# Attention scores of two heads as alternating 64-row fp32 matmuls, with queries and keys kept as one fp32 copy

## The chip, the cores and the metric

The kernel runs on one core of one Trainium2 chip. The metric is the device time of one execution in microseconds (us). Five engines work beside each other, each through its own queue in order: TensorE (PE in the profile; its weight loads are shown apart as PEld), VectorE (DVE), ScalarE (ACT), GpSimd (POOL) and SyncE (SP, which only issues DMA transfers here). They wait for one another by semaphores.

## The reference, cut to what matters

One inference step of a decoder layer: a normalised input is projected by one matrix, its columns are split into a mixer A (windowed attention, 6 heads of 64) and a mixer B (mLSTM, 4 heads of 160), the two outputs go through one output projection, and a feed-forward network follows. 2048 prompt positions and 8 single-token samples are computed. The change touches mixer A on the prompt:

```python
s = jnp.einsum('bnqrhe,bnkrhe->bnrhqk', qb, kc).astype(jnp.float32) * scale + bias
s = jnp.where(mask[None, :, None, None], s, NEG)
lse = jax.nn.logsumexp(s, axis=-1)
p = jnp.exp(s - lse[..., None]).astype(v.dtype)
o = jnp.einsum('bnrhqk,bnkrhe->bnqrhe', p, vc).reshape(B, s_pad, H, E)[:, :S]
...
o = jnp.stack([b[0] for b in branches])
w = jax.nn.softmax(lse, axis=0).astype(o.dtype)
return jnp.einsum('gbsh,gbshe->bshe', w, o)
```

Every head is computed for three branches, (window, dilation) = (128, 1), (512, 4) and (2048, 16). In each, 128 queries that lie `dilation` positions apart see the 128 keys of their own block and, where there is one, the 128 keys of the block before. All inputs and outputs are fp32.

## The kernel before

The program is recorded in Python and a list scheduler then puts each engine's instructions into a fixed order, by priority and by its own estimate of when operands are ready. So work of several stages is interleaved on PE, but the order is fixed when the program is built. The stages that matter:

- **Normalisation and values** (`norm_and_v`, L770): tile by tile, x is normalised and transposed, and the value columns and gates are projected. The values go to a DRAM buffer `v_d` laid out head by head, with a column of ones behind each head's 64 (L863).
- **Projection of keys and queries** (`project_qk`, L909): for each of three column blocks (two heads each) and six blocks of positions, 24 matmuls on split operands (`mm3`, L161: a high and a low fp32r part of each operand) fill a PSUM tile `pmm`. The tile is copied to `qb` by ACT, and split again into `qhi` (ACT) and `qlo` (DVE, L159 for keys, L956 for queries). Each goes to its own DRAM buffer (L962). Keys are also transposed (`to_rows`, L913) for the output `p_k` through a tile `kt`. Between the column blocks, `setup_bias` (L235) writes the bias table to DRAM by a broadcast to 128 rows (L252), and `setup_gates` (L260) makes the gate sums; its PE transpose of `u` (L284) needs DVE's `u` (L282).
- **Second half of the projection for mixer B with attention** (`xbob(1)`, L1160): for each of its 15 blocks, six steps of the generator `attention` are recorded. PE's projection matmuls here are the groups called `pmm` at L162 to L164.
- **mLSTM with attention** (`mlstm`, L1167): 16 chunks, each a chain through PE, DVE, ACT and POOL; attention's remaining steps are recorded between them by a fixed ratio (L1229). When attention is done, the output weights are loaded there too.
- **Output projection and feed-forward network** (`phase_c`), after 1060 us, not touched.

Attention before works on one head at a time. `load_head` (L1042) loads `Q2`, which holds the high parts of a head's 64 query columns in rows 0 to 63 and the low parts in rows 64 to 127; `KH` and `KL`, which hold the high (low) parts of its keys twice. `front` (L1058) makes scores for two query blocks of the head: for each, two fp32r matmuls over all 128 rows and 256 columns, Q2 with KH and Q2 with KL, which add up in `ps_s` (L1073). The fp32r form is run with 256 columns even where only 128 keys count. For the branches with dilation 4 and 16 both operands are read with that stride. DVE adds the bias and takes the row minimum (L1075), ACT takes the exponential (L1077). `turn` (L1080) transposes the 128x128 blocks on PE, `weigh` (L1094) multiplies them with the values into `po`, ACT copies `po` to a row tile `R4` (L1103), and SP stores it. In what follows a **head-tile** is the scores of 128 queries of one head in one branch: 6 heads x 3 branches x 16 = 288 of them, 576 matmuls. `ps_s` has two buffers of one PSUM bank, each with two head-tiles.

fp32 matmuls stand in the profile as two PE records each (and two weight loads); fp32r matmuls and transposes as one.

## Time and profile before

| what | value |
|---|---|
| time, median of 3 runs | 2720.37 us (2719.04 to 2722.34) |
| span of the profiled execution | 2721.4 us |
| busy share of PE, DVE, ACT, POOL | 97%, 54%, 31%, 7% |
| matmul records at L1073 (scores) | 576, from 400.8 to 938.7 us |
| matmul records at L1101 (weighing with values), L1086 (transposes) | 900 and 450 |
| DMA packets | 334227, of these 108543 under 512 B |

The profiled execution's own time is taken as its span of 2721.4 us; it lies 1.0 us above the median of the three runs. A matmul's recorded duration reaches into the next ones, since matmuls are pipelined, so what one costs is read from the distance between the starts of successive records, not from its duration.

### The profile page before, as it was taken

To read this page: it belongs to the slowest core of one execution; us is meant where nothing else is said; L and a number is where in the kernel's file an instruction comes from. 1 tells how busy PE (TensorE), PEld (TensorE's weight loads), DVE (VectorE), ACT (ScalarE), POOL (GpSimd) and SP (SyncE) were. 2 spreads that over 40 slices of the span, in tenths; PEclk is the share of its full clock that TensorE was granted. 3 is DMA by queue.
4 is the path that set the end of the run, shared out by engine and by line. 5 is a ranking of instruction groups with operands and counts; after the bars stand their busy time and mean duration, and the time that the engine had idled before them with its cause. 6 is when DMAs were issued, how large, how long until landed. Compare 5 with 4: busy or idle time off the path is not lost.

```text
span 2721.4 us, 39886 instructions
## 1 busy us (share of the span) xinstructions
PE 2650.5 (97%) x15366; PEld 2355.4 (87%) x15366; DVE 1469.2 (54%) x3444; ACT 846.1 (31%) x1898; POOL 202.7 (7%) x198
## 2 busy tenths in 40 slices
PE   8999999999999979999999999999999999999997
PEld 7999999999798867887888888888899999999996
DVE  6324655666477575753344444544754545454547
ACT  5321224444445443322321212121452121212123
POOL 1000000000344243110000000000000000000001
PEclk9999999999799979999999999999999999999998
DMA  8675566656476565543222312111241111111113
GB/s 196 152 196 163 167 171 142 152 140 159 129 185 169 145 189 159 174 152 125 70 97 66 101 63 62 46 55 40 93 155 55 39 55 39 55 40 55 40 38 119
DMA packets 334227, 302.57 MB, mean 111 GB/s; under 512 B 108543, under 2 KB 301467, under 8 KB 331092
## 3 DMA queue, kind: packets, MB, share of 16 engines
q1 hardware_dynamic: 332212, 296.39, 38.6%
q0 software_dynamic: 1536, 3.10, 0.5%
q8 instruction: 121, 1.98, 0.3%
q14 instruction: 70, 0.57, 0.1%
q10 hardware_dynamic: 288, 0.53, 0.1%
HBM read 220.94 MB, written 95.17 MB: 116 GB/s over the span
## 4 chain that ended last, share of the span: by engine, by line
PE 88%; DVE 4%; DMA 4%; ACT 2%; issue 1%; POOL 1%; SPq 0%; DVEq 0%; POOLq 0%; ACTq 0%
PE pf L163 19%; PE pf L162 19%; PE pf L164 19%; PE pmm L162 5%; PE pmm L164 5%; PE pmm L163 5%; PE ps_s L1073 4%; PE po L1101 3%; PE pt L1086 2%; PE ptp L176 1%; PE ppq L162 1%; PE up L437 1%; DMA tr_d<-tb_d 0%; PE ppq L164 0%; PE nu L458 0%
## 5 line engine op out<-in xcount | busy, mean ns | idle before, releaser
L1442 DVE TENSOR_TENSOR acc<-acc,pf 128x512 f32<-128x512 f32 (+2 forms) x600 | 343.1, 581 | 201.5 <-PE pf L164 200.2
L164 PE MATMUL pf<-rh,w2l 128*128 128x512 f32 (+2 forms) x1280 | 445.4, 348 | 0.0
L163 PE MATMUL pf<-rlo,w2h 128*128 128x512 f32 (+2 forms) x1280 | 445.0, 348 | 0.1
L162 PE MATMUL pf<-rh,w2h 128*128 128x512 f32 (+2 forms) x1280 | 444.4, 347 | 0.0
L162 PEld LDWEIGHTS pf<-rh,w2h 128*128 128x128 f32 x1280 | 241.8, 189 | 30.2 <-ACT rh L158 0.2
L163 PEld LDWEIGHTS pf<-rlo,w2h 128*128 128x128 f32 x1280 | 241.4, 189 | 30.6 <-DVE rlo L159 0.3
L164 PEld LDWEIGHTS pf<-rh,w2l 128*128 128x128 f32 x1280 | 241.3, 189 | 30.0 <-DVE w2l L159 0.2
L162 PE MATMUL pmm<-x,wh 128*128 128x344 f32 (+1 forms) x768 | 251.3, 327 | 0.0
L163 PE MATMUL pmm<-x,wh 128*128 128x344 f32 (+1 forms) x768 | 249.3, 325 | 0.0
L164 PE MATMUL pmm<-x,wl 128*128 128x344 f32 (+1 forms) x768 | 248.7, 324 | 0.0
L162 PE MATMUL pf<-h21h,w1h 128*128 128x512 f32 (+2 forms) x768 | 245.8, 320 | 0.0
L164 PE MATMUL pf<-h21h,w1l 128*128 128x512 f32 (+2 forms) x768 | 245.6, 320 | 0.0
L163 PE MATMUL pf<-h21l,w1h 128*128 128x512 f32 (+2 forms) x768 | 245.2, 319 | 0.0
L158 ACT ACTIVATE rh<-rl 128x264 fp32r<-128x264 f32 (+1 forms) x160 | 87.1, 545 | 465.9 <-PE pf L164 278.9
L163 PE MATMUL pf<-h20l,w1h 128*128 128x512 f32 x512 | 200.0, 391 | 0.0
L162 PE MATMUL pf<-h20h,w1h 128*128 128x512 f32 x512 | 199.9, 390 | 0.0
L164 PE MATMUL pf<-h20h,w1l 128*128 128x512 f32 x512 | 199.4, 390 | 0.0
L159 DVE TENSOR_TENSOR w1l<-w1r,w1h 128x1024 fp32r<-128x1024 f32 x64 | 78.4, 1225 | 184.7 <-ACT w1h L158 184.7
L1077 ACT ACTIVATE ex<-sm,R 128x256 f32<-128x256 f32 (+1 forms) x288 | 125.9, 457 | 145.4 <-DVE R L1075 140.9
L1421 DVE TENSOR_TENSOR rl<-rl 128x264 f32<-128x264 f32 (+1 forms) x160 | 93.2, 583 | 141.4 <-ACT rl L1420 141.4
L1075 DVE CUSTOM_DVE_ANT_0 sm<-ps_s,nb 128x256 f32<-128x256 f32 (+1 forms) x288 | 99.7, 362 | 118.4 <-PE ps_s L1073 88.9
L163 PEld LDWEIGHTS pf<-h21l,w1h 128*128 128x128 f32 x768 | 144.6, 188 | 12.8
(471 smaller groups left out, 5171.0 us busy)
## 6 DMA issues: line engine op xcount, KB each, us to landing
w1r<-in_w_ff_dram SPq DMA_DIRECT2D x64, 512.0 KB
w2r<-in_w_ff_dram SPq DMA_DIRECT2D x64, 512.0 KB
xt<-in_x_prompt_dram SPq DMA_DIRECT2D x31, 512.0 KB
xt<-x_d SPq DMA_DIRECT2D x25, 512.0 KB
R_d<-R SPq DMA_DIRECT2D x72, 132.0 KB
Rb<-R_d SPq DMA_DIRECT2D x48, 198.0 KB
V<-v_d SPq DMA_DIRECT2D x72, 130.0 KB
wraw<-in_w_in_dram SPq DMA_DIRECT2D x17, 512.0 KB
```

Of the source, the lines that this page charges most:

```text
L158: last_hi[0] = act.activation(hi, src, AF.Copy)
L159: last_lo[0] = (eng or vec).tensor_tensor(lo, src, hi.bitcast(F32), op=OP.subtract)
L162: pe.matmul(out, lh, rh, start=first, stop=False)
L163: pe.matmul(out, lh, rl, start=False, stop=False)
L164: pe.matmul(out, ll, rh, start=False, stop=last)
L1073: pe.matmul(out, Q[:, a:a + (P - 1) * d + 1:d], mv, start=i == 0, stop=i == 1)
L1075: vec.tensor_tensor_reduce(sm[:, :w], s_[:, e, c0:c0 + w], nb[:, o + bw - w:o + bw], 1.0, 3e38, OP.add, OP.min, mn)
L1077: act.activation(ex[:, e, :w], sm[:, :w], AF.Exp, bias=mn, scale=-1.0)
L1086: pe.transpose(pt[:, e, kb], ex[:, e, kb * P:(kb + 1) * P], ident)
L1101: pe.matmul(po[:, i + e], pT[:, e, kb], vts[kb], start=kb == 0, stop=kb == nk - 1)
L1421: vec.tensor_tensor(r[:, :n], r[:, :n], r[:, :n], op=OP.mult)
L1442: vec.tensor_tensor(av, av, pf[:, :n], op=OP.add)
```

## The change

Queries and keys are no longer split for attention. `project_qk` copies each PSUM block once (queries with the scale -0.125) and stores it once, in one fp32 buffer `q_d` and one `k_d`. Their 128 rows per column block are two heads, 64 rows each. Attention takes the two heads of a column block as a pair: `load_pair` loads both heads' rows as they lie. For each query block, one fp32 matmul over rows 0 to 63 makes the first head's scores and one over rows 64 to 127 the second head's. The two write different PSUM banks, and they are recorded alternately. The matmuls have 128 columns where only 128 keys count, else 256. All 288 head-tiles are now one fp32 matmul each, 288 in place of 576.

A step makes two query blocks of two heads, in two `ps_s` buffers, so both buffers are taken in every step. `flush` is now a generator: it does one head of the pair, yields, and does the other. The lag between scores and transposes is one step (`DEPTH` 1) of double size. Values lie position by position in `v_d`, so that a pair's columns are read as pieces of 520 B; results are stored per step as pieces of 528 B in place of 264 B. The number of DVE, ACT and PE instructions per head-tile behind the scores stays as it was.

```diff
-    q_d = [dram.tile([DA, S], F32, name=f"q{x}_d") for x in "hl"]
-    k_d = [dram.tile([DA, S], F32, name=f"k{x}_d") for x in "hl"]
-    v_d = dram.tile([HA, S, HD + 1], F32, name="v_d")
+    q_d = dram.tile([DA, S], F32, name="q_d")
+    k_d = dram.tile([DA, S], F32, name="k_d")
+    v_d = dram.tile([S, VW], F32, name="v_d")
...
-                    hi = ev.tile([P, 344], F32R, name="qhi")
-                    lo = ev.tile([P, 344], F32R, name="qlo")
-                    if which == "k":
-                        qb = ev.tile([P, 344], F32, name="qb", bufs=3)
-                        act.activation(qb[:, :n], ps[:, :n], AF.Copy)
-                        split(hi[:, :n], lo[:, :n], qb[:, :n])
-                    else:
-                        act.activation(hi[:, :n], ps[:, :n], AF.Copy, scale=-0.125)
-                        vec.scalar_tensor_tensor(lo[:, :n], ps[:, :n], -0.125, hi[:, :n].bitcast(F32),
-                                                 op0=OP.mult, op1=OP.subtract)
...
-                    for dd, tt in zip(dst, (hi, lo)):
-                        nc.sync.dma_start(dd[j * P:(j + 1) * P, b0:b0 + m], tt[:, :m].bitcast(F32))
+                    qb = ev.tile([P, 344], F32, name="qb", bufs=3)
+                    act.activation(qb[:, :n], ps[:, :n], AF.Copy, scale=1.0 if which == "k" else -0.125)
+                    nc.sync.dma_start(dst[j * P:(j + 1) * P, b0:b0 + m], qb[:, :m])
...
-            Q, KH, KL = (wk.tile([P, S], F32, name=x) for x in ("Q2", "KH", "KL"))
-            for dst, lo, hi in ((Q, q_d[0], q_d[1]), (KH, k_d[0], k_d[0]), (KL, k_d[1], k_d[1])):
-                nc.sync.dma_start(dst[:HD], lo[hs])
-                nc.sync.dma_start(dst[HD:], hi[hs])
+            Q, K = (wk.tile([P, S], F32, name=x) for x in ("Q2", "K2"))
+            nc.sync.dma_start(Q, q_d[j * P:(j + 1) * P])
+            nc.sync.dma_start(K, k_d[j * P:(j + 1) * P])
...
-            s_ = ps.tile([P, 2, 256], F32, name="ps_s", tag="s", bufs=2)
-            for e, (a, w, mn, vts) in enumerate(tiles):
-                for i, K in enumerate((KH, KL)):
...
-                    pe.matmul(out, Q[:, a:a + (P - 1) * d + 1:d], mv, start=i == 0, stop=i == 1)
+            s_ = [ps.tile([P, 2, 256], F32, name="ps_s", tag="s", bufs=2) for _ in range(2)]
+            for t, (a, w, _, _) in enumerate(tiles):
+                k0 = a - (w - P) * d
+                for e in range(2):
+                    hs = slice(HD * e, HD * e + HD)
+                    pe.matmul(s_[e][:, t, :w], Q[hs, a:a + (P - 1) * d + 1:d],
+                              K[hs, k0:k0 + (w - 1) * d + 1:d], start=True, stop=True)
...
-        pend, turned, acc_o, DEPTH = [], [], [None], 2
+        nxt = load_pair(0)
+        pend, turned, acc_o, DEPTH = [], [], [None], 1
...
-                    V = wk.tile([P, 4, HD + 1], F32, name="V", bufs=4)
-                    nc.sync.dma_start(V, rows(v_d, b, g, HD + 1, h * S * (HD + 1), HD + 1))
-                    R4 = wk.tile([P, 4, HD + 2], F32, name="R4", bufs=3)
+                    V = wk.tile([P, 4, 2, HD + 1], F32, name="V", bufs=4)
+                    nc.sync.dma_start(V.rearrange("p t e c -> p t (e c)"),
+                                      rows(v_d, b, g, 0, VW, 2 * j * (HD + 1), 2 * (HD + 1)))
                     for i in (0, 2):
+                        R2 = wk.tile([P, 2, 2, HD + 2], F32, name="R2", bufs=4)
```

Where this moves instructions is shown in three places. The first is PE's queue in the stage where attention runs beside the projection for mixer B. Before, in the first head's steps with dilation 4, score matmuls (L1073) stand in pairs of KH and KL between projection matmuls (`pmm`) and transposes (`pt`):

```order
L1073 MATMUL ps_s<-KH,Q_4213 128x256
L1073 MATMUL ps_s<-KL,Q_4213 128x256
L1086 MATMUL pt<-ident,ex 128x128 x4
L163 MATMUL pmm<-x_115,wh 128x344
L1073 MATMUL ps_s<-KH,Q_4213 128x256
L1073 MATMUL ps_s<-KL,Q_4213 128x256
L164 MATMUL pmm<-x_114,wl 128x344
L1073 MATMUL ps_s<-KH,Q_4213 128x256
L1073 MATMUL ps_s<-KL,Q_4213 128x256
L1086 MATMUL pt<-ident,ex 128x128 x4
```

With the change, in the first pair's steps with dilation 4, four score matmuls (now L1055, two query blocks of two heads) stand together, and the steps follow each other in bursts, with transposes (L1072) and value matmuls (`po`, L1087) between:

```order
L1055 MATMUL ps_s<-K_4065,Q_4064 128x256 x4
L1087 MATMUL po<-V,pT 128x65 x4
L1072 MATMUL pt<-ident,ex 128x128 x4
L1087 MATMUL po<-V,pT 128x65 x4
L1072 MATMUL pt<-ident,ex 128x128 x4
L1055 MATMUL ps_s<-K_4065,Q_4064 128x256 x4
L1087 MATMUL po<-V,pT 128x65 x4
L1072 MATMUL pt<-ident,ex 128x128 x4
```

What moved: the score matmuls of a step now form one run, with nothing of another form in it. In all, the projection stage (up to PE's last `pmm` matmul) has 49 such runs with 168 score matmuls in place of 336, 128 of them with strided operands; 27 of the runs are a full alternation of four.

The second place is PE's queue in the mLSTM stage, in the last pair, where the scheduler could not keep the four together (`up`, `psA` and `pt<-ident,cp` are the mLSTM's own):

```order
L1055 MATMUL ps_s<-K_6769,Q_6768 128x256
L416 MATMUL pt<-ident,cp 128x128 x4
L1055 MATMUL ps_s<-K_6769,Q_6768 128x256
L418 MATMUL pt<-ident,cp 128x128
L1072 MATMUL pt<-ident,ex 128x128 x2
L1055 MATMUL ps_s<-K_6769,Q_6768 128x256
L437 MATMUL up<-v_7214,cw 128x161 x3
L439 MATMUL up<-v_7214,cw 128x161
L441 MATMUL up<-v_7214,cw 32x161 x4
L1055 MATMUL ps_s<-K_6769,Q_6768 128x256
```

What moved: here a 64-row matmul stands alone between others four times in one step. This stage has 54 runs with 120 score matmuls (64 strided) in place of 240; 12 runs are a full alternation, and 21 are a single matmul.

The third place is DVE's queue in the projection of keys, ahead of `u`. Before, four low parts (`qlo`) stand between the gates' `lf` and the copies that `u` needs:

```order
L330 SCALAR_TENSOR_TENSOR lf<-gat,ls_ab 128x64
L159 TENSOR_TENSOR qlo<-qb,qhi 128x340 x2
L159 TENSOR_TENSOR qlo<-qb,qhi 128x344 x2
L280 COPY a<-ptp 128x64
L281 COPY bt<-ptp 128x64
L282 TENSOR_TENSOR u<-gat,a 128x64
```

With the change nothing stands between them:

```order
L327 SCALAR_TENSOR_TENSOR ls_ab<-gat 128x64
L933 COPY qs_1478<-ptp 8x128
L330 SCALAR_TENSOR_TENSOR lf<-gat,ls_ab 128x64
L280 COPY a<-ptp 128x64
L281 COPY bt<-ptp 128x64
L282 TENSOR_TENSOR u<-gat,a 128x64
```

What moved: `u` no longer stands behind `qlo`, which is gone.

More of the change, by code (lines that the diff above doesn't have):

```diff
@@ L862, in norm_and_v @@
             if t < NT:
[L863 removed]
+                nc.sync.dma_start(v_d[c0:c0 + P], vt.rearrange("p h e -> p (h e)"))
                 nc.sync.dma_start(O["p_v"][0, 0, c0:c0 + P], vt[:, :, :HD])
@@ L1060, in front, with rows @@
+        def rows(t, b, g, i, rs, off, w):
+            st = ((rs, P * rs), (4 * rs, rs), (16 * rs, rs))[b]
+            row = (512 * g + P * i, 512 * g + i, 4 * g + i)[b]
+            n = 4 if t is v_d else 2
+            return bass.AP(tensor=t.tensor, offset=t.offset + row * rs + off, ap=[[st[0], P], [st[1], n], [1, w]])
+        def front(pair, b, tiles):
+            nb, Q, K = pair
             d = BRANCHES[b][1]
             o, bw = NBW[b]
-            ex = wk.tile([P, 2, 256], F32, name="ex", bufs=3)
@@ L1097, in weigh @@
             po = acc_o[0]
[L1098 removed]
+            for t, (_, w, _, vts) in enumerate(tiles):
                 nk = w // P
                 for kb in range(nk):
[L1101 to L1107 removed]
@@ L1109, in flush @@
-        def flush():
-            if len(turned) == 1:
-                weigh(*turned.pop(0))
-            if pend:
-                tiles, ex, *rest = pend.pop(0)
-                turned.append((tiles, turn(tiles, ex), *rest))
-        for h in range(HA):
-            cur = hd
+                    pe.matmul(po[:, t, e], pT[:, t, kb], vts[kb][:, e], start=kb == 0, stop=kb == nk - 1)
+            if e:
+                act.activation(R2[:, :, :, :HD + 1], po, AF.Copy)
+                nc.sync.dma_start(dst, R2.rearrange("p t e c -> p t (e c)"))
@@ new lines, in attention @@
+        nxt = load_pair(0)
+        pend, turned, acc_o, DEPTH = [], [], [None], 1
+        def flush():
+            old = turned.pop(0) if turned else None
+            new = pend.pop(0) if len(pend) > DEPTH or not live[0] and pend else None
+            pTs = []
+            for e in range(2):
+                if old is not None:
+                    tiles, pT, *rest = old
+                    weigh(tiles, pT[e], e, *rest)
+                if new is not None:
+                    pTs.append(turn(new[0], new[1], e))
+                if e == 0:
+                    yield
+            if new is not None:
+                turned.append((new[0], pTs, *new[2:]))
```

83 lines of the change are left out of this document (34 added, 49 removed).

## Prediction

> **What bounds the kernel now.** I read the page's busy shares first, then its chain of waits, then a table by stage.
>
> ```profile
> PE 2650.5 (97%) x15366; PEld 2355.4 (87%) x15366; DVE 1469.2 (54%) x3444; ACT 846.1 (31%) x1898; POOL 202.7 (7%) x198
> ...
> PE 88%; DVE 4%; DMA 4%; ACT 2%; issue 1%; POOL 1%; SPq 0%; DVEq 0%; POOLq 0%; ACTq 0%
> ```
>
> PE is busy 97% of the span and carries 88% of the chain: time is mostly PE's. The table by stage (columns: stretch, its length, busy time and count on PE, PEld, DVE, ACT, POOL, then the granted clock, DMA share, GB/s) has the projections up to 398 in two pieces, then attention beside the projection for mixer B (398 to 658), then attention inside the mLSTM (658 to 945).
>
> ```profile
> core 0: us, PE busy (x) PEld busy (x) DVE busy (x) ACT busy (x) POOL busy (x), PEclk, DMA share, GB/s
> 130.00:200.00 70.00, 64.30 (x402) 61.33 (x401) 21.30 (x78) 20.92 (x61) 1.13 (x5) 0.95 0.73 189
> 200.00:398.00 198.00, 197.25 (x1295) 196.29 (x1294) 109.49 (x258) 47.50 (x90) 0.00 (x0) 1.00 0.57 164
> 398.00:658.00 260.00, 259.76 (x1705) 251.25 (x1704) 156.79 (x600) 108.61 (x257) 0.95 (x3) 1.00 0.65 150
> 658.00:945.00 287.00, 271.79 (x1849) 242.47 (x1846) 185.44 (x599) 135.96 (x405) 104.67 (x96) 0.93 0.61 158
> ```
>
> In the first attention stage PE is idle 0.2 us of 260: what PE saves there is saved whole. In the second it is idle 15 of 287, at a mean clock of 0.93, so something else also sets the end. The chain of the first attention stage, by line and with one of its longest pieces:
>
> ```profile
> by line: PE ps_s L1073 31.5%; PE po L1101 19.0%; PE pmm L163 12.9%; PE pmm L164 12.8%; PE pmm L162 12.8%; PE pt L1086 10.5%; DVE g1t L1028 0.5%; PE ptp L1011 0.2%; issue 0.2%; DVE R L1075 0.0%; DVE sm L1075 0.0%
> 457.77 1.51 PE po L1101 x14
> ```
>
> Scores (L1073) are 31.5% of 260 us, 82 us. Their records in the two stages:
>
> ```profile
> 398.00:658.00 260.00, 104.18 (x338) 77.59 (x338) 1.00 0.65 150
> 658.00:945.00 287.00, 78.77 (x238) 52.85 (x238) 0.93 0.61 158
> ```
>
> 338 records are 169 head-tiles of two matmuls, so 0.48 us each. What a pair costs depends on its operands. First a pair with neighbouring columns (dilation 1), then two pairs with a stride, from the timeline of PE (start, duration, instruction, count):
>
> ```profile
> 449.03 0.33 PE L1101 MATMUL po<-V,pT 128*128 128x65 f32 x2
> 449.17 0.36 PE L1073 MATMUL ps_s<-KH,Q 128*128 128x256 f32 x1
> 449.37 0.28 PE L1073 MATMUL ps_s<-KL,Q 128*128 128x256 f32 x1
> 449.49 0.60 PE L1086 MATMUL pt<-ident,ex 128*128 128x128 f32 x4
> ```
> ```profile
> 426.82 0.45 PE L1073 MATMUL ps_s<-KH,Q 128*128 128x256 f32 x1
> 427.08 0.42 PE L1073 MATMUL ps_s<-KL,Q 128*128 128x256 f32 x1
> 427.32 0.42 PE L1073 MATMUL ps_s<-KH,Q 128*128 128x256 f32 x1
> 427.56 0.41 PE L1073 MATMUL ps_s<-KL,Q 128*128 128x256 f32 x1
> 427.80 0.29 PE L1086 MATMUL pt<-ident,ex 128*128 128x128 f32 x1
> ```
>
> From 449.03 to 449.49 PE starts two `po` records and one score pair: 0.46 us. `po` alone takes 0.11 each (14 in 1.51 us, above), which leaves 0.24 for the pair. The strided pairs take 0.98 us for two, 0.49 each; where the strided weight load meets a short `po` matmul it is more, and I take 0.51. That a stride doubles a matmul (0.24 against 0.12) is the change's lever.
>
> **The score matmuls now.** No row shows a 64-row fp32 matmul with a stride. The nearest ones are the mLSTM's fp32 matmuls on column groups and its 32-row matmuls. First the former: `up` with 128 columns (L437), four heads' matmuls on 32 columns each (L441), and what follows.
>
> ```profile
> 740.56 0.99 PE L437 MATMUL up<-v,cw 128*128 128x161 f32 x6
> 741.38 0.44 PE L439 MATMUL up<-v,cw 128*128 128x161 f32 x2
> 741.75 0.16 PEld L441 LDWEIGHTS up<-v,cw 128*32 128x32 f32 x8 [0.17 <-DVE hss L470]
> 741.75 0.48 PE L441 MATMUL up<-v,cw 128*32 128x161 f32 x8
> 742.16 0.32 PE L1101 MATMUL po<-V,pT 128*128 128x65 f32 x1
> ```
>
> L437's six records start 0.137 us apart for 161 columns, which is 0.218 for 256 and 0.109 for 128. L441's eight records, four heads with two each, are over 0.41 us after their start (741.75 to 742.16); one behind the other they would need 1.1 us. So matmuls in different parts of the array overlap wholly, at least by column groups. I take the same for two row groups. The other bound is no overlap.
>
> For one fp32 record over 256 strided keys I take 0.22: at 0.137 us for 161 columns it asks for a value every 0.85 ns anyway, about as slowly as the strided fp32r matmul gets them (0.24 us for 256). That is the lower bound; if the record reads its keys twice, it is 2 x 0.24 = 0.48. I take the lower, since it is the pace that fp32 rows have. Over 128 strided keys the weight load sets the pace: `po`'s records of 65 columns come 0.11 apart, a load's time, and a strided load is about 0.1 longer (below), so again 0.22. Hence a **slot** (one matmul, two records; the other head's runs beside it) is 0.44 us strided, 0.43 for 256 neighbouring keys.
>
> Against this stands the change of form. In the mLSTM, 32-row matmuls follow 128-row ones:
>
> ```profile
> 744.09 0.28 PE L164 MATMUL ppq<-cph,MTm 128*128 128x256 f32 x1
> 744.30 0.38 PE L162 MATMUL ppq<-cph,MTm 32*128 32x256 f32 x1
> 744.53 0.28 PE L163 MATMUL ppq<-cpl,MTm 32*128 32x256 f32 x1
> 744.65 0.28 PE L164 MATMUL ppq<-cph,MTm 32*128 32x256 f32 x1
> 744.86 0.39 PE L162 MATMUL ppq<-cph,MTm 128*128 128x256 f32 x1
> ```
>
> Within a form the records start 0.12 us apart; at each change two starts are late, 744.09 to 744.30 and to 744.53, then again from 744.65, about 0.21 us more in all per change: PE drains, and the next weight load is not covered. A run of score matmuls pays this on entry and on exit: 0.42. With a strided first load it pays about 0.10 more, by the weight loads' median against their least (min/median/max):
>
> ```profile
> L1073 PEld LDWEIGHTS ps_s<-KL,Q x288: 186/310/352, 407.3 to 938.6; 128*128 128x128 f32 x144
> ```
>
> So a run costs 0.42 (neighbouring) or 0.52 (strided), plus its slots; slots are counted as the larger of the two heads' numbers in a run. From the built order:
> - First stage, 168 score matmuls: 38 strided runs and 11 others, 76 and 22 slots: 19.8 + 4.6 + 33.4 + 9.5 = 67.3 us. Before, 128 strided at 0.51 and 40 others at 0.24: 74.9, or 82 by the chain, which charges load waits to scores that `po` would have in part anyway. Gain 7.6 to 14.6; I take **-10**.
> - Second stage, 120 matmuls in 54 broken runs: 28 strided and 26 others, 41 and 37 slots: 14.6 + 10.9 + 18.0 + 15.9 = 59.4. Before, 64 at 0.51 and 56 at 0.24: 46.1, or 52 by the dearer count (0.32 from 449.17 to 449.49, and 0.53). So PE's work *grows* by 8 to 13 us, 10 in the middle. How much of it counts, the chain of this stage says:
>
> ```profile
> by line: PE ps_s L1073 8.7%; PE po L1101 6.9%; issue 6.4%; PE ppq L162 5.6%; PE up L437 4.8%; PE pt L1086 4.0%; PE ppq L164 3.1%; PE nu L458 3.0%; PE ppq L163 3.0%; PE nu L460 2.6%; PE nu L461 2.6%; PE psA L408 2.3%; PE psA L409 2.2%; DVE h
> ...
> 804.13 5.67 DMA wr<-wsT_d
> 822.89 6.94 DMA cp<-cT_d
> ```
>
> Scores are 8.7% of 402 us, 35 us, against 119 x 0.48 = 57 of PE's time: six tenths of what is added here lands on the end. **+6.5** (0 to +13).
>
> So a complete step of dilation 1 loses (0.42 + 2 x 0.43 = 1.28 against 4 x 0.24), steps with a stride win (0.52 + 2 x 0.44 = 1.40 against 4 x 0.51), and where the scheduler breaks a step up, it loses again.
>
> **Waits added.** Both `ps_s` buffers are taken in each step, so a step's first score matmul waits for DVE's reads of the step before, and on PE everything queues behind it. DVE's two costs in the first stage are
>
> ```profile
> L1075 DVE CUSTOM_DVE_ANT_0 sm<-ps_s,nb 128x256 f32<-128x256 f32 x100 | 40.2, 421 | 38.0 <-PE ps_s L1073 29.1 <-ACT R L1103 3.1 <-PE pt L1086 2.1
> L1088 DVE COPY pT<-pt 128x512 f32<-128x512 f32 x45 | 30.9, 687 | 7.2 <-PE pt L1086 6.9
> ```
>
> In the bursts of the built order, a full step has 1.4 us of scores, 16 value records and 8 transposes at 0.11 on PE: 4.0 us. DVE has four reads at 0.42, a short accumulator read behind each, and two copies at 0.69: 3.1 to 3.4. PE is the slower one and covers the wait; +1 (0 to +10: in the mLSTM, DVE's queue also holds the chunk's operations).
>
> **The projection of keys and queries.** PE is the bound here (197.25 of 198 us), so the removed splits on ACT and DVE and the halved stores give nothing in general: PE hides them. But one stall rests on them. A row of DVE, one of ACT, then the wait of PE:
>
> ```profile
> 157.01 0.52 DVE L159 TENSOR_TENSOR qlo<-qb,qhi 128x340 fp32r<-128x340 f32 x1 [16.39 <-DMA kl_d<-qlo]
> ...
> 157.53 0.38 ACT L924 ACTIVATE kt<-ptp 128x256 f32<-128x256 f32 x1 [5.99 <-DMA out_dram<-kt]
> ...
> PE ptp L284 <- DVE u L282: 4.6, 1, 4.6
> ```
>
> `qlo` waits 16.4 us for its buffer, whose store has not landed (the bias broadcast of L252 is under way); `u` stands behind it in DVE's queue, PE's transpose of `u` behind that: 4.6 us idle. And the clock falls: 0.95 over 70 us, 3.5 us lost. With `qlo` gone, `u` comes as soon as PE's gate sums are there. `qb` now waits for its own store, but has three buffers, and four PSUM tiles stand behind it. **-8** (0 if ACT, which waits 6.0 us for a store of `kt` as before, lets PSUM run full).
>
> **DMA.** Keys and queries are loaded as 6 MB in place of 18 (Q2, KH and KL 12 loads each, of 512 KB); the pieces of values and results grow:
>
> ```profile
> KH<-kh_d SPq DMA_DIRECT2D x12, 512.0 KB
> ```
>
> Where DMA stands on the path (the two pieces of 5.7 and 6.9 us above), some contention goes: a quarter of their 12.6 us, -3 (0 to -10).
>
> **Sum.** 2721.4 - 10 + 6.5 + 1 - 8 - 3 = 2707.9 for the profiled execution. It lies 1.0 above the median, so **2707**, 0.5% faster. PE's transposes, value matmuls and DVE's work stay as they are.
>
> **A rule that speaks against it.** The L441 rows show all eight weight loads done 0.16 us after the first began, while the first four matmuls still run (PEld row), so a group's next load is hidden behind its own matmul. The Trainium skill, "TensorE: Matmul & The Clock Gate", Part 3 (what overlaps and what doesn't), says that weight loads overlap with running matmuls only where the row groups differ. By it each head's loads and streams would alternate. The trace speaks against it, for column groups; by that rule the time would be the last rival's 2750, by the trace 2707.
>
> **Rivals.**
> - *The two heads do not overlap* (the slower side). Unlike L441 the groups here split rows. Slots become 168 and 120 instead of 98 and 78: +70 x 0.44 = 31 and +42 x 0.44 x 0.6 = 11; **2749**. It decides against the change once over a third of the overlap is missing (14 of 42 us). For: no row shows it; against: L441. 12%.
> - *Strided keys are read twice*: 51 slots over 256 strided keys (31 and 20) cost 0.48 more: +15 and +6, **2728**. For: fp32r showed that a stride halves the reading. 18%.
> - *The stall in the projection only changes its cause* (`kt` for `qlo`): +8, **2715**. For: ACT's wait for `kt` in the same 16 us. 12%.
> - *The mLSTM absorbs the added work and DMA's relief is large*: -6.5 and -7, **2693**. 8%.
> - *Each head's loads and streams alternate*: a record costs load plus stream, 0.15 more on average; 2 x (98 + 0.6 x 78) x 0.15 = 43: **2750**. 3%.
>
> My forecast has 47%, with 2695 to 2720 as its own range.
>
> **Range and chances.** 2683 to 2746 takes in all but no overlap and its like (15%) and a little on the fast side. About 0.2% (5.4 us) is what a measurement of this kernel can tell from no change. Faster: four fifths of the forecast, the 8%, and a little of the others, 0.46; within 0.2%: the rest of the forecast's range, most of the unmoved stall, 0.20; slower: re-reading, no overlap, alternation, 0.34.
>
> **What would show it.** In the new profile, L1055's records should start in pairs a few ns apart, with the step over in about 0.9 us after its first load; a step of dilation 1 and one of dilation 4 should take nearly the same. At 0.22 against 0.48 between a head's records, reading once or twice shows. The stretch up to PE's last `pmm` should be some 18 us shorter, about 8 of it before 200 us, with no clock fall near 160 us; the mLSTM stretch some 5 us longer. I am wrong if L1055's second head starts only after the first ends, or if PE waits for `ps_s` in the bursts.

## The result, and the profile after

The changed kernel takes **2754.36 us** (median of 4 runs, 2753.27 to 2757.70) against 2720.23 us of the kernel before (4 runs, 2719.04 to 2722.34): ratio 1.0125, 95% interval 1.0108 to 1.0141. It is 1.25% slower, where 0.5% faster was forecast, and it lies beyond the upper end of the range (2746). The profiled execution has a span of 2752.0 us, 30.6 more than before. Two executions of the later runs, one of run 5 and one of the kernel before beside runs 8 and 9, took about 5130 us and are left out of all figures below.

The page of the changed kernel, its busy shares and its table of time slices (the granted clock in tenths):

```profile
PE 2688.0 (98%) x15366; PEld 2338.5 (85%) x15366; DVE 1460.5 (53%) x3408; ACT 831.7 (30%) x1877; POOL 204.8 (7%) x198
...
PEclk9999999989788989999999999999999999999998
```

PE is busier than before (2688.0 against 2650.5 us) with as many records, and the slices in which the clock falls, the last one apart, have grown from two to five. The table by stage of the changed kernel, same columns and stretches as in the prediction:

```profile
130.00:200.00 70.00, 67.11 (x442) 65.89 (x442) 12.85 (x60) 16.51 (x50) 1.13 (x5) 1.00 0.63 164
200.00:398.00 198.00, 194.28 (x1267) 191.99 (x1265) 103.60 (x257) 49.11 (x94) 0.00 (x0) 0.99 0.53 155
398.00:658.00 260.00, 259.18 (x1631) 227.94 (x1631) 150.11 (x575) 99.39 (x246) 0.00 (x0) 0.93 0.36 105
658.00:945.00 287.00, 279.72 (x1704) 223.65 (x1703) 177.81 (x557) 123.44 (x372) 98.41 (x90) 0.85 0.47 134
```

Up to 200 us the forecast gain is there: the clock is 1.00 where it was 0.95, and the first score starts at 391.6 us instead of 400.8. In the two attention stages PE is as busy as before, but the third column from the end, the granted clock, is 0.93 where it was 1.00, and 0.85 where it was 0.93. A busy share says nothing of this.

The clock records of the trace hold two values, 1.0 and 0.5, in pieces that are multiples of 3.41 us. So I count the time at half clock, and take half of it off the span: what the program would last if PE had always had its full clock (the span times the mean clock says nearly the same: 2752.0 x 0.968 = 2664). It is an estimate, and too high a price, since not everything slows down with the clock. Repeated executions of one program, which get different clocks, give another: over 103 executions of the kernels in this document, each compared with the others of the same kernel in the same run, the span grows by 0.40 us (0.36 to 0.44) for each us at half clock, reckoned as twice the span times (1 - mean clock); one execution of run 2 with a mean clock of 0.931 at an ordinary time is left out. "Stage 1" is the stretch from the first score to PE's last `pmm`, "stage 2" from there to the mLSTM's last `psA`; half-clock time of each in brackets.

| kernel | span us | half clock us | span less half of it | stage 1 | stage 2 |
|---|---|---|---|---|---|
| before | 2721.4 | 90.3 | 2676.2 | 255.8 (0.0) | 377.8 (68.3) |
| after | 2752.0 | 174.9 | 2664.6 | 273.5 (41.0) | 401.6 (119.5) |

Counted by the halves, as in the table, the change would have gained 11.6 us at full clock and lost 42.3 (half of 84.6) to the clock. Counted by 0.40 it lost 34 and would have gained 3. Either way, the clock is the whole of the loss; what the change is worth without it is 3 to 12 us.

**The scores themselves.** The timeline of PE in the changed kernel: a step of dilation 4, then one of dilation 1, then two half steps of dilation 4 that the scheduler separated (start, duration, instruction, count of records):

```profile
467.76 2.20 PE L1055 MATMUL ps_s<-K,Q 64*128 64x256 f32 x8
469.89 0.88 PE L1087 MATMUL po<-V,pT 128*128 128x65 f32 x6
...
495.76 1.13 PE L1055 MATMUL ps_s<-K,Q 64*128 64x256 f32 x8
496.83 1.11 PE L1087 MATMUL po<-V,pT 128*128 128x65 f32 x8
...
602.66 2.19 PE L1055 MATMUL ps_s<-K,Q 64*128 64x256 f32 x4
604.78 0.33 PE L1072 MATMUL pt<-ident,ex 128*128 128x128 f32 x1
605.04 2.19 PE L1055 MATMUL ps_s<-K,Q 64*128 64x256 f32 x4
607.16 1.14 PE L1087 MATMUL po<-V,pT 128*128 128x65 f32 x6
```

Eight records over neighbouring keys take 1.07 us to the next start, eight strided ones 2.13. One head alone (four records at 602.66) takes as long as two heads, 2.12: so the two heads do run beside each other, and a strided record takes twice as long whether or not the other head is there. And here the clock falls. The table by stretch of the same place:

```profile
604.20:607.60 3.40, 3.40 (x11) 1.74 (x9) 1.00 (x5) 0.91 (x2) 0.00 (x0) 1.00 0.40 88
607.65:614.40 6.75, 6.75 (x32) 5.48 (x32) 3.42 (x15) 3.39 (x8) 0.00 (x0) 0.50 0.09 24
```

PE is busy 3.40 of 3.40 us, with 11 records, of which six are scores, of one head at a time; in the next 6.75 us it has half its clock. What that costs stands a little later in the same half-clock stretch, in the projection's own matmuls, which the change leaves as they are:

```profile
614.88 0.49 PE L163 MATMUL pmm<-x,wh 128*128 128x344 f32 x1
615.16 0.49 PE L164 MATMUL pmm<-x,wl 128*128 128x344 f32 x1
615.45 0.49 PE L162 MATMUL pmm<-x,wh 128*128 128x344 f32 x1
```

They start 0.29 us apart; at full clock the median in this stage is 0.16. Over the whole of stage 1, PE's time from the starts of these matmuls to the next start is 117.3 us, where it was 107.4 before.

### The profile page after: what moved, and what is told of

The parts are those of the page before. It is cut to its first block, busy times and chain, and to the rows that moved or that the text cites. A ratio compares the mean times of both kernels' runs of the same rounds, so it can differ in the third digit from the quotient of the medians.

```text
span 2752.0 us, 39582 instructions
## 1 busy us (share of the span) xinstructions
PE 2688.0 (98%) x15366; PEld 2338.5 (85%) x15366; DVE 1460.5 (53%) x3408; ACT 831.7 (30%) x1877; POOL 204.8 (7%) x198
## 4 chain that ended last, share of the span: by engine, by line
PE 89%; DVE 5%; DMA 3%; ACT 2%; issue 1%; POOL 0%; SPq 0%; ACTq 0%; DVEq 0%; POOLq 0%
PE pf L163 19%; PE pf L164 19%; PE pf L162 19%; PE pmm L162 5%; PE pmm L164 5%; PE pmm L163 5%; PE ps_s L1055 4%; PE po L1087 4%; PE pt L1072 2%; PE ppq L162 1%; PE ptp L176 1%; PE up L437 1%; PE ppq L164 1%; PE ppq L163 1%; DMA out_dram<-kt 1%
## 5 line engine op out<-in xcount | busy, mean ns | idle before, releaser
L162 PEld LDWEIGHTS pf<-h21h,w1h 128*128 128x128 f32 x768 | 144.4, 188 | 12.0
L164 PEld LDWEIGHTS pf<-h21h,w1l 128*128 128x128 f32 x768 | 144.4, 188 | 11.1
```

What stands on the lines that cost most here:

```text
L162: pe.matmul(out, lh, rh, start=first, stop=False)
L164: pe.matmul(out, ll, rh, start=False, stop=last)
```

## The experiments

Theory A: the clock is granted by how much of the array has streamed in a window of 3.41 us, so bursts of attention (64 rows, strided, 65 columns, paced by weight loads) between blocks of projection matmuls halve it. Rivals: waits on PE, since both `ps_s` buffers are taken in each step (W); dearer scores (S).

**1. What the clock makes of each form.** Eleven stretches of one kind of matmul each, with full-width ones between; the core of it:

```diff
+    warm()
+    for _ in range(28):
+        mm(o[0][:, :256], A[lo, 0:509:4], B[lo, 0:1021:4])
+    warm()
+    for _ in range(28):
+        mm(o[0][:, :256], A[lo, 0:509:4], B[lo, 0:1021:4])
+        mm(o[1][:, :256], A[hi, 0:509:4], B[hi, 0:1021:4])
...
```

> Not the model's computation: eleven stretches of matmuls of one kind on PE, some 24 us each, with full-width fp32r matmuls (128 rows, 512 columns) between them; the outputs hold nothing. In order: (1) one head, 64 rows, fp32, 256 neighbouring columns; (2) the same, stride 4; (3) two heads on the two row groups, stride 4; (4) two heads, neighbouring; (5) 128 rows, fp32, stride 4; (6) 128 rows, 65 columns; (7) transposes; (8) one head, 128 neighbouring columns; (9) 128 rows, fp32r, stride 4; (10) 32 rows, fp32r; (11) one 128-row fp32 matmul and one pair of 64-row ones in turn. Theory A (the clock weighs streamed columns by the part of the array they use, and halves below about 0.3 in a window of 3.4 us): (1) is at 0.48, (3) and (5) 0.46, (4) 0.97, (6) and (8) 0.49, (9) 0.44: all keep 1.0; (2) at 0.23 and (10) at 0.25 fall to 0.5. Theory B (rows do not count): (2) at 0.46 and (10) at 1.0 keep the clock too. Theory C (a half-empty array loses): (1), (2), (8), (10) fall. Costs: if a stride makes fp32 records read at half pace whatever runs beside them, (2), (3), (5) have 0.45 to 0.48 us per record, (1) and (4) 0.22; if the two heads' reading side by side is slow, only (3) has 0.46. In (11) each change of form costs 0.2 us by the prediction, a round 1.28 us; without such a cost 0.86.

The table by stretch of this kernel, one row for each of the eleven (PE's records in brackets; the clock is the third column from the end):

```profile
42.00:66.00 24.00, 24.00 (x112) 20.70 (x112) 0.00 (x0) 0.00 (x0) 0.00 (x0) 1.00 0.00 1
81.00:105.50 24.50, 24.50 (x55) 16.31 (x54) 0.00 (x0) 0.00 (x0) 0.00 (x0) 0.57 0.00 1
122.00:146.00 24.00, 24.00 (x108) 16.35 (x106) 0.00 (x0) 0.00 (x0) 0.00 (x0) 1.00 0.00 1
162.00:184.50 22.50, 22.50 (x212) 20.28 (x210) 0.00 (x0) 0.00 (x0) 0.00 (x0) 1.00 0.00 1
200.00:223.50 23.50, 23.50 (x52) 15.89 (x52) 0.00 (x0) 0.00 (x0) 0.00 (x0) 1.00 0.00 0
239.00:262.00 23.00, 23.00 (x209) 23.00 (x207) 0.00 (x0) 0.00 (x0) 0.00 (x0) 1.00 0.00 1
277.00:297.50 20.50, 20.50 (x190) 20.50 (x189) 0.00 (x0) 0.00 (x0) 0.00 (x0) 1.00 0.00 1
313.00:336.00 23.00, 23.00 (x208) 23.00 (x207) 0.00 (x0) 0.00 (x0) 0.00 (x0) 1.00 0.00 1
351.50:373.50 22.00, 22.00 (x95) 22.00 (x94) 0.00 (x0) 0.00 (x0) 0.00 (x0) 1.00 0.00 1
389.00:427.00 38.00, 38.00 (x191) 38.00 (x191) 0.00 (x0) 0.00 (x0) 0.00 (x0) 0.54 0.00 1
445.00:473.00 28.00, 28.00 (x135) 13.41 (x134) 0.00 (x0) 0.00 (x0) 0.00 (x0) 1.00 0.00 1
```

PE is 100% busy in all rows, and exactly the two that theory A names fall: one head over strided keys (second row), and 32 rows at full pace (tenth). The same strided records of two heads side by side (third) keep the clock. Rows count, then, and so does the pace; by the weights of the expectation the limit lies between 0.25 (fell) and 0.44 (ninth row, held). Theories B and C are out. The Trainium skill, "TensorE: Matmul & The Clock Gate", Part 1 (the HAM clock gate), puts the half rate down to an idle window of about 3.4 us; the window's length agrees (3.41), the idleness does not: the second row has none.

The paces, from the starts of successive records: neighbouring 0.217 us (one head), 0.108 (two heads together); strided 0.461 (one head), 0.229 (two), 0.457 (128 rows). So two heads overlap wholly, and a stride costs fp32 a factor of two, whatever runs beside it. The strided records of one head stand 0.458 us apart in the median both before the clock falls (10 records) and after it (45), so half clock does not slow them; the 32-row records go from 0.120 to 0.213. A round of one 128-row matmul and one pair takes 1.26 us, from PE's timeline:

```profile
443.82 0.59 PE L82 MATMUL big<-B,A 128*128 128x256 f32 x2
444.34 0.70 PE L82 MATMUL o<-B,A 64*128 64x256 f32 x4
444.98 0.70 PE L82 MATMUL big<-B,A 128*128 128x256 f32 x2
445.60 0.70 PE L82 MATMUL o<-B,A 64*128 64x256 f32 x4
446.24 0.70 PE L82 MATMUL big<-B,A 128*128 128x256 f32 x2
```

From 444.98 to 446.24 is 1.26, four records' paces are 0.87: 0.2 us per change of form, as predicted.

With the paces of the traces one can weigh each window of 3.41 us of a whole kernel between 380 and 1075 us: every record's columns at its form's full pace (0.217 us for 256 columns in fp32, transposes included; 0.117 in fp32r, from the 0.157 between the projection's records of 344), put at the end of the record and multiplied by its share of the array's 128 rows, over 3.41 us. In the changed kernel the 17 windows ahead of a fall have 0.11 to 0.39, and the 139 after which the clock held have 0.40 and more. In the repetition (run 9) the 18 falls have 0.15 to 0.395, the 135 others 0.398 and more. Over the twelve profiles of whole kernels in this document, a border of 0.395 leaves 13 of 2013 windows on the wrong side. Without the share of rows even the best border leaves 39 there; with the share of the array's columns multiplied in as well as that of the rows, 29. So it is rows and pace that count here; the columns' share does not, as far as the few matmuls on fewer than 128 columns of the array can tell.

**2. The same instructions in another order.** The steps recorded between the projection's matmuls instead of behind them:

```diff
+            if tick[0] is not None and k in (1, 3, 5):
+                next(tick[0], None)
...
-    for _ in xbob(1, ps, "n", ps):
-        for _ in range(6):
-            next(att, None)
+    tick[0] = att
+    for _ in xbob(1, ps, "n", ps):
+        pass
```

> The changed kernel with the same instructions; only the place of the attention steps beside the mixer-B projection differs: instead of three whole steps recorded behind each block of 48 projection matmuls, half a step is recorded after every six of them. Theory A (the lost time is the clock: bursts of attention without projection matmuls between them leave windows of 3.4 us with too little streamed, and PE is halved): half-clock time from the first score to the last pmm falls from 41 us to under 7, this stretch from 273.5 us to 253 to 258, and the whole to 2733 to 2742 us. Theory W (the lost time is waits on PE: both ps_s buffers taken, changes of form, transposes waiting for exponentials): half-clock time falls too or not, but the stretch falls by no more than the 7 us of waits, the whole to 2747 or more. Theory S (64-row scores are simply dearer): no change, 2754.

2726.61 us (10 runs), ratio to before 1.0025 (1.0004 to 1.0046). The two stages of this kernel:

```profile
393.20:654.70 261.50, 261.45 (x1802) 230.58 (x1802) 164.49 (x638) 109.76 (x271) 0.00 (x0) 0.97 0.40 117
654.70:1037.40 382.70, 351.22 (x2243) 287.75 (x2243) 247.76 (x725) 172.78 (x527) 140.20 (x127) 0.88 0.51 148
```

28 us came back by order alone: 12 in stage 1 (half-clock time 41.0 to 13.7 us) and 19 in the mLSTM, which has less attention left (216 score records instead of 240), less 1.6 by which the first score comes later. Half-clock time falls by 51 us in all, worth 26 by the halves and 21 by 0.40. At full clock, then, this kernel is 3 to 8 us shorter than the changed one: W's share is that at most. S falls. Theory A's figures came in part: the whole is below the 2733 to 2742 expected, but stage 1 has 13.7 us of half clock and not under 7, and lasts 261.4 us and not 253 to 258, with 7% more attention in it.

**3. The stride.** Keys of dilation 4 copied into neighbouring columns by ScalarE:

```diff
-                    pe.matmul(s_[e][:, t, :w], Q[hs, a:a + (P - 1) * d + 1:d],
-                              K[hs, k0:k0 + (w - 1) * d + 1:d], start=True, stop=True)
+                    keys = K4[0][hs, k0 % 4, k0 // 4:k0 // 4 + w] if b == 1 else K[hs, k0:k0 + (w - 1) * d + 1:d]
+                    pe.matmul(s_[e][:, t, :w], Q[hs, a:a + (P - 1) * d + 1:d], keys, start=True, stop=True)
...
-            for b in (2, 1, 0):
+            for b in (2, 0, 1):
...
+                    if b == 0 and g == 2:
+                        K4[0] = wk.tile([P, 4, 512], F32, name="K4", tag="K2")
+                        for r in range(4):
+                            act.activation(K4[0][:, r], cur[2][:, r:r + 4 * 511 + 1:4], AF.Copy)
```

> The changed kernel with a copy of the keys in the order of dilation 4, made by ScalarE in SBUF (four copies of 512 columns per pair of heads), so that the dilation-4 scores read neighbouring keys; the branches run in the order 16, 1, 4 instead of 16, 4, 1 so that the copy finds a free buffer. Theory A with the stride's price (records over 256 strided keys take 0.46 us against 0.22): 31 slots x 0.48 = 15 us of PE's time go in the first stage and 20 x 0.48 x 0.6 = 6 on the path in the mLSTM; ScalarE's 12 copies cost it some 7 us that PE hides. Fewer windows fall to half clock, since the strided steps are those that stream least. 2754 goes to 2725 to 2738. Theory S (it is the two heads' reading beside each other, or the weight loads, that make the records 0.46): the slots of dilation 4 stay at 0.9 us and the time within 5 us of 2754. If half-clock time in the first stage stays near 41 us while the records get short, the clock is not a matter of the strided records.

2713.98 us (10 runs), ratio 0.9965 (0.9943 to 0.9987): faster than the 2725 to 2738 expected. The branches also run in another order here, which was not tried alone. A step of dilation 4 takes 1.24 us, from 499.84 to 501.08 in PE's timeline, instead of 2.13:

```profile
499.84 1.31 PE L1056 MATMUL ps_s<-K,Q 64*128 64x256 f32 x8
501.08 0.66 PE L1087 MATMUL po<-V,pT 128*128 128x65 f32 x4
```

Scores take 14.5 us less in stage 1 and 12.9 less in stage 2, and half-clock time falls to 140.5: records that stream faster also keep the clock.

**4. Not alternating.** Both tiles of one head first, then of the other:

```diff
-            for t, (a, w, _, _) in enumerate(tiles):
-                k0 = a - (w - P) * d
-                for e in range(2):
+            for e in range(2):
+                for t, (a, w, _, _) in enumerate(tiles):
+                    k0 = a - (w - P) * d
```

> The changed kernel with the score matmuls of a step in another order: both tiles of the first head, then both of the second, in place of alternating heads. If the alternation buys what the change is for (two heads side by side in the array), it is lost for all but the middle of a step: a step over 256 neighbouring keys goes from 1.06 us to about 1.7, with a stride from 2.1 to about 3.7; 14 to 30 us more in the first stage, 2775 to 2800 in all. If two heads do not in fact gain from each other, or the engine takes matmuls of another row group out of turn, the time stays within 5 us of 2754. By the clock theory half-clock time grows beyond 41 us in the first stage, since one head alone uses half the array.

2774.81 us (one run), but not for the reason expected: the steps take as long as before, here 2.13 us for a strided one, and the two heads' records start 14 ns apart (7 ns where they alternate).

```profile
469.85 2.20 PE L1055 MATMUL ps_s<-K,Q 64*128 64x256 f32 x8
471.98 0.77 PE L1087 MATMUL po<-V,pT 128*128 128x65 f32 x5
```

The engine runs the two row groups beside each other though in the built order both matmuls of the first head stand ahead of the second head's. The time is half clock again: 211.1 us, and 2667.6 by the halves, 3 from the changed kernel. Why more windows fall here was not followed up; the changed kernel itself differs by 16 us of half clock between its two profiles (run 9).

**5. Both edits together.**

> The changed kernel with both edits: half a step of attention recorded after every six projection matmuls, and the keys of dilation 4 copied into neighbouring columns by ScalarE (branches in the order 16, 1, 4). Theory A (clock, plus the stride's price): the copy takes some 15 us off PE's scores in the first stage, the spreading takes the half-clock time left there (17.1 us with the copy alone) to under 7; the two gains share the clock's part (about 12 us), so against 2754 the 28 of the one and the 40 of the other give 50 to 60 together: 2694 to 2706, faster than the kernel before. If the two were independent, 2686; if both gained by the same thing, 2714 as with the copy alone.

**2705.34 us** (3 runs, 2705.04 to 2708.34), ratio 0.993 (0.9908 to 0.9952): the best measured, 0.7% faster than before and at the upper end of the 2694 to 2706 expected. Half-clock time in stage 1 is 10.2 us, not under 7, and in the mLSTM still 102.4.

**6 and 7. The kernel before, with parts.** Four buffers for the split parts in the projection:

```diff
-                    hi = ev.tile([P, 344], F32R, name="qhi")
-                    lo = ev.tile([P, 344], F32R, name="qlo")
+                    hi = ev.tile([P, 344], F32R, name="qhi", bufs=4)
+                    lo = ev.tile([P, 344], F32R, name="qlo", bufs=4)
```

> The kernel before the change with one edit: four buffers instead of two for qhi and qlo in the projection of keys and queries. It separates the projection's part of the change. If the stall at 157 to 161 us hangs on qlo's buffer alone, as the prediction had it, the fall of the clock at 160 us is gone and the first score comes some 9 us earlier (391 to 393 instead of 400.8), the whole 8 to 10 us shorter than before: 2710 to 2714 against 2720 to 2723. If another store takes its place (kt), the time is within 3 us of before.

2731.22 us (10 runs), ratio 1.0032 (1.0018 to 1.0045): both expectations missed. PE's waits in this kernel (us in total, times, longest):

```profile
PE pt L577 <- DVE W L574: 7.9, 1, 7.9
PE ptp L284 <- DVE u L282: 3.1, 1, 3.1
```

The wait for `u` is 3.1 us instead of 4.6, and its reason is the next one in line, a row of ACT's timeline:

```profile
156.49 0.38 ACT L924 ACTIVATE kt<-ptp 128x256 f32<-128x256 f32 x1 [6.31 <-DMA out_dram<-kt]
```

ACT waits 6.31 us for a store of `kt`; `qhi` stands behind it, `qlo` behind `qhi`, `u` behind `qlo`. And a new wait of 7.9 us has come up in the samples' attention, with 24 us of half clock ahead of the first score. So the buffer alone wasn't it. In the changed kernel ACT waits for a store of `kt` too, and longer, as a row of its timeline says:

```profile
151.18 0.38 ACT L924 ACTIVATE kt<-ptp 128x256 f32<-128x256 f32 x1 [8.73 <-DMA out_dram<-kt]
```

But `qlo` is gone from DVE's queue, nothing there hands this wait on to `u`, and PE has no wait for `u` (its longest between 130 and 200 us is 1.9, for `qb`). That speaks for the splits as the cause and not for the halved stores; no run changed one without the other. Why L574 comes late was not followed further.

With the copy of both parts of the keys besides:

```diff
...
+                    if b == 0 and g == 2:
+                        for n, x in enumerate(("KH", "KL")):
+                            K4[n] = wk.tile([P, 4, 512], F32R, name=x + "4", tag=x)
+                            for r in range(4):
+                                act.activation(K4[n][:, r], cur[2 + n][:, r:r + 4 * 511 + 1:4].bitcast(F32), AF.Copy)
```

> The kernel before the change with the four buffers and with the copy of the dilation-4 keys (both fp32r parts, eight copies of 512 columns per head by ScalarE, branches in the order 16, 1, 4): 128-row fp32r scores as before, one head at a time, now over neighbouring keys. If what costs is the stride and not the form, a strided head-tile goes from 0.51 to 0.24 us: 62 of them in the first stage give 16 us, 40 in the mLSTM 10 x 0.6 = 6, besides the 9 of the projection: some 2690 (2685 to 2698). A pair of 64-row slots then has nothing left to win: 0.43 for two head-tiles and 0.4 us of changes of form per run, against 0.48. If this is slower than the spread version of the changed kernel with the same copy, the two-head form is worth something beyond the stride; if it is faster or the same, it is not.

2742.86 us (5 runs), ratio 1.0057 (1.0037 to 1.0077), a miss: the score records stay 0.23 us apart with neighbouring keys. PE's weight loads in this kernel point to the reason:

```profile
460.36 0.31 PEld L1080 LDWEIGHTS ps_s<-KH,Q 128*128 128x128 f32 x1
460.57 0.33 PEld L1080 LDWEIGHTS ps_s<-KL,Q 128*128 128x128 f32 x1
460.80 0.33 PEld L1080 LDWEIGHTS ps_s<-KH,Q 128*128 128x128 f32 x1
```

The loads of the strided queries come at the same pace as the records, 0.21 to 0.23 us; that they set it is shown by run 11. The prediction had put the 0.24 us down to the keys.

**8 and 9. More work for the clock.** Two dummy matmuls behind each half step's value matmuls, and the changed kernel itself on the same chip:

```diff
+            for _ in range(2):
+                pe.matmul(acc_o[0][:, 260:512], fill[:, :P], fill[:, :252], start=True, stop=True)
```

> The changed kernel with more work and nothing else: behind the value matmuls of each half step stand two dummy fp32r matmuls of 252 columns and 128 rows, into the unused part of the po bank, 288 in all. By the 0.12 us between fp32r records they add some 34 us to PE. Theory A (the clock): they put 0.42 us of full-array streaming into each step of some 4 us, which lifts most windows that are now between 0.2 and 0.3 over the limit; half-clock time up to the last psA falls from 160 us to under 110, which gives 25 us or more back, and the time is 2750 to 2765 in place of 2754 + 34. Span less half of the half-clock time, which is 2672 for the changed kernel, becomes some 2700. Any theory in which PE is long because of waits or dearer records: half-clock time does not move, or it does not matter, and the time is 2780 or more.

> The changed kernel itself once more, on the same chip as the kernel with dummy matmuls, so that the two are compared side by side: 2750 to 2758, half-clock time 41 us in the first attention stage and about 120 in the mLSTM.

The changed kernel took 2754.45 us again (4 runs), with the dummies 2773.53 (4 runs): 19 more, against 34 of added work as expected, or 42 by the fourth column of the table below (2705.4 less 2663). It lies between the two expectations: the clock gave some of it back, less than I had put. In stage 1 the case is clean: half-clock time 10.2 us instead of 27.3 to 41.0, and a length of 274.6 us against 266.4 to 273.5, with 160 dummies of 0.12 us (19 us) in it. The repetition also tells something by itself. It did not get the half clock expected of it (27.3 and 143.4 us, where 41 and about 120 were). Stage 1 had 13.7 us less than in the first profile and was 7.1 us shorter; the mLSTM had 23.9 us more and was 9.3 us longer (410.9). Program and order are the same, so this is the clock's price in the mLSTM as well: 0.39 us for each us at half clock, and 0.52 in stage 1.

**10 and 11. Queries in order as well**, in the best version and in the kernel before:

```diff
+                        Q4[0] = wk.tile([P, 4, 512], F32, name="Q4", tag="Q2")
...
+                            act.activation(Q4[0][:, r], cur[1][:, r:r + 4 * 511 + 1:4], AF.Copy)
```

> The spread version of the changed kernel with the dilation-4 keys copied, and now the dilation-4 queries copied into neighbouring columns too (four more copies of 512 columns per pair by ScalarE). The copy of the keys alone left a dilation-4 step of eight records at 1.24 us against 1.06 for neighbouring keys and queries. Where the strided load of queries is what remains, these steps go to 1.06: some 28 whole steps x 0.18 = 5 us of PE, of which 3 to 5 show: 2701 to 2705 against 2706.8. If ScalarE's copies make the exponentials late, it is 2707 or more.

2707.70 us (4 runs), ratio 0.993 (0.9905 to 0.9956): no more gain, where 2701 to 2705 was expected if the loads were all that remained; scores take 2.3 us less in stage 1, and half-clock time is 144.8 us against 128.3.

In the kernel before, with its own buffers:

```diff
-                    pe.matmul(out, Q[:, a:a + (P - 1) * d + 1:d], mv, start=i == 0, stop=i == 1)
+                    qs = K4[0][:, a % 4, a // 4:a // 4 + P] if b == 1 else Q[:, a:a + (P - 1) * d + 1:d]
+                    pe.matmul(out, qs, mv, start=i == 0, stop=i == 1)
```

> The kernel before the change (its own buffers) with keys and queries of dilation 4 in neighbouring columns (twelve copies of 512 columns per head by ScalarE, branches in the order 16, 1, 4). With the keys alone in order a record still took 0.233 us, the pace of the strided load of queries (0.33 us each). Theory L (the load sets the pace of the fp32r form): with both in order a head-tile of dilation 4 falls from 0.49 to 0.24 us, score time in the first stage from 79 to some 62 us, the time by 12 to 20 us to 2703 to 2711: nearly what the two-head form with the same copies gives, so that form would be worth little by itself. Theory R (the moving operand or something else sets it): the records stay at 0.23, the time 2720 or more. If the 72 copies of ScalarE and the waits for them eat the gain, score time falls to 62 but the stage does not.

2747.05 us (4 runs), ratio 1.0076 (1.0053 to 1.0099), far from theory L's 2703 to 2711. For the records theory L holds: with queries and keys in order, four of them take 0.56 us, from 507.47 to 508.03 in PE's timeline.

```profile
507.47 0.36 PE L1081 MATMUL ps_s<-KH,Q 128*128 128x256 f32 x1
507.67 0.28 PE L1081 MATMUL ps_s<-KL,Q 128*128 128x256 f32 x1
507.79 0.28 PE L1081 MATMUL ps_s<-KH,Q 128*128 128x256 f32 x1
507.90 0.28 PE L1081 MATMUL ps_s<-KL,Q 128*128 128x256 f32 x1
508.03 0.38 PE L1094 MATMUL pt<-ident,ex 128*128 128x128 f32 x2
```

Scores take 64.0 us in stage 1 (78.9 before), which is 11 us shorter, 244.5. But the mLSTM is 30 us longer, with half-clock time 119.5 and this wait of PE:

```profile
PE ps_s L1081 <- DVE R L1083: 32.8, 9, 14.1
```

That it comes from ScalarE's 72 copies is likely but was not shown. In the stage where PE alone is the bound, then, 128-row fp32r scores over neighbouring columns do as well as two heads side by side (249.4 us in run 5, which had 7% more attention in its stage 1).

The whole kernels of these runs in one table:

| kernel | span | half clock | span less half of it | stage 1 | stage 2 |
|---|---|---|---|---|---|
| 2 spread | 2723.5 | 123.6 | 2661.7 | 261.4 (13.7) | 382.7 (92.2) |
| 3 keys in order | 2718.2 | 140.5 | 2648.0 | 249.8 (17.1) | 387.2 (102.4) |
| 4 not alternating | 2773.1 | 211.1 | 2667.6 | 277.5 (51.2) | 417.7 (143.4) |
| 5 = 2 + 3 | 2706.6 | 128.3 | 2642.5 | 249.4 (10.2) | 378.1 (102.4) |
| 6 before, buffers | 2735.3 | 110.4 | 2680.1 | 256.1 (0.0) | 380.1 (75.1) |
| 7 before, buffers, keys | 2755.0 | 147.9 | 2681.0 | 254.5 (3.4) | 397.9 (102.4) |
| 8 dummies | 2769.2 | 127.4 | 2705.4 | 274.6 (10.2) | 414.0 (99.0) |
| 9 after again | 2757.9 | 190.9 | 2662.4 | 266.4 (27.3) | 410.9 (143.4) |
| 10 queries too | 2711.1 | 144.8 | 2638.7 | 250.3 (20.5) | 378.9 (105.8) |
| 11 before, both | 2740.7 | 140.9 | 2670.3 | 244.5 (3.4) | 407.5 (119.5) |

The changed kernel, its repetition and the two with its instructions in another order (2 and 4) differ by 50 us in span and by 6 in the fourth column.

## Why the prediction was wrong, step by step

- **The step that failed** is the first one: "what PE saves there is saved whole", a sum in microseconds of PE at a clock taken as given. The clock was read in the profile (1.00 and 0.93), charged once for the stall at 160 us, and had no term for the change. That term is +34 to +42 us: 41 us of half clock in the first stage and 51 more in the mLSTM, less 7 at the stall, at 0.40 to 0.5 each. None of the rivals named it, and neither sign by which the prediction meant to be found wrong came up: the second head's records start 7 ns behind the first's, and PE waits for DVE's reads of `ps_s` only once, 0.9 us, in the two stages. The term is shown for stage 1 by runs 1 and 2, and for both stages by the weights of the windows and by the two profiles of one program (run 9).
- Without the clock the sum was -13.5 with 3.5 of clock at the stall, so -10.0. Measured it is -11.6 by the halves and -3 by 0.40. Where it comes near, that is in part luck, since errors cancel in it, as follows (start-to-start times, half of those at half clock taken off, which flatters the changed kernel).
- **First stage, -10 and +1.** Scores -13.2 (78.9 to 65.7). Two heads overlap and a change of form costs 0.2: right. *Strided keys are read twice*, which I gave 18%, is right in its price where there are 256 of them (0.46 per record); whether they are read twice or at half pace no run shows. It is hidden in that sum because other runs were cheaper than 1.28 to 1.40, with 1.07 and, over 128 keys, 1.16. "PE's transposes, value matmuls and DVE's work stay as they are" is wrong: +11.3 (69.6 to 80.9). Standing together they come 0.110 us apart on average, where before, between projection matmuls, it was 0.095 (that weight loads pace them was not tested); a start ahead of a run of scores comes 0.1 later. By the halves the stage gains 2.8 at full clock, not 9; by 0.40 it gains nothing.
- **Second stage, +6.5**: by the halves it is 1.7 us shorter at full clock (343.6 to 341.9) and the terms were too dear by 8; by 0.40 it is 3 us longer. This is too coarse to judge the term by.
- **DMA, -3**: the two pieces that it rests on (5.67 and 6.94 us) are gone from the mLSTM's chain, on which one DMA piece is left (5.03 us). Whether that is relief or PE being longer, no run separates.
- **The stall, -8**: the first score comes 9.2 us earlier, right; its cause was more than `qlo`'s buffer: the whole chain from `kt` through `qhi` and `qlo` to `u` (run 6).
- **What I said would show it**: pairs start a few ns apart, there is no fall at 160 us, and a dilation-4 step does not take the time of a dilation-1 step. The stretch up to the last `pmm` became 8 us longer instead of 18 shorter.

## What to carry to other kernels

Where PE is 100% busy, read the granted clock by stage before adding up microseconds, and ask of each change what it makes of the streaming in a window of 3.4 us: fewer rows, strided operands, short moving operands and order count, not busy time. In these kernels the clock halved when less than about 0.39 of a window was filled, by full pace and rows. Mix weak forms (few rows, few columns, paced by loads) with full matmuls every few microseconds rather than behind blocks of them; here that alone was worth 28 us. Before giving up a form for its cost with a stride, find out which operand sets the pace, by putting one of them in order at a time.

## What was not expected of the hardware

- The clock halves with PE busy without a gap, when 64 rows stream at half pace (0.461 us per 256 columns) or 32 rows at full pace; 128 rows at the same half pace hold it. In whole kernels the border lies between 0.39 and 0.40 of a window of 3.41 us, counted by pace and rows, with transposes as streaming.
- At half clock the projection's records go from 0.16 to 0.29 us, while the strided 64-row fp32 record stays at 0.458.
- Two row groups run beside each other, 14 ns apart, though one head's two matmuls stand ahead of the other's in the queue.
- The fp32 matmul and the fp32r matmul lose a factor of two to a stride by different operands: the fp32 record by its moving operand (2.13 to 1.24 us per step with the keys in order), the fp32r record by its weight load (0.23 us with the keys in order; four records in 0.56 with both).
